# Even mixer: sixteen attention heads as one stream, with the query and key products of each pair of heads woven in

## The chip, the core and the metric

The kernel runs on one core of one Trainium2 chip. The metric is the device time of one execution in microseconds (us). Engines are named as in the profile: PE is TensorE's matmul part and PEld its weight loads, DVE is VectorE, ACT is ScalarE, POOL is GpSimd, SP is SyncE, which here issues nearly all DMAs. Each engine works off its own instructions in the order of the program.

## The reference, cut to what matters

The reference runs a differential attention block with mixture of experts, then two layers with a mixer and a feed-forward each. The change lies in the mixer of the first of these layers (the even mixer), for 512 tokens of width 1024. It projects the normed input once (`even_w_in`) and attends with two sets of eight heads of width 64:

```
q_a, k_a, v_a, q_idx, k_idx, w_idx, q_b, k_b, v_b = split(x @ w_in)
# A: sparse attention. An index score picks 128 keys for each query, softmax over those alone
score = sum_h relu(q_idx[h] . k_idx) * w_idx[h]            # 4 index heads
keep  = top_k(score, 128), within the allowed chunks
o_a   = softmax(where(keep, q_a . k_a / 8, -1e30)) @ v_a    # 8 heads, rotary q and k
# B: chunked attention with a relative position bias
o_b   = softmax(q_b . k_b / 8 + rel_bias) @ v_b             # 8 heads
h     = h + concat(o_a, o_b) @ w_out
```

All arithmetic is in float32 precision. Products are made in three passes of halves (high by high, low by high, high by low).

## The kernel before

Eight stages follow each other; `stage_c` is the even mixer, from about 620 to 941 us of the profiled execution. The stage `stage_e` (the odd mixer, later) uses the same helper for its softmax heads.

**Products.** `fm` makes tiles of 128 outputs x 512 tokens; a tile of the input projection is 8 k-chunks x 3 passes = 24 matmuls of 512 columns into one `mm` buffer of PSUM, one of `w_out` 4 x 3 = 12. The weights are loaded (`wr`), cast to a high half on ACT (`wh`, L110) and the low half is subtracted on DVE (`wl`, L111). `tm` makes the value tiles with the tokens as rows. All these come as lists of units, each with a cost; `weave` merges two lists by cost, `emit` runs a list. What is emitted is then ordered by a list scheduler, which can move an instruction ahead on its engine where it takes it to be ready sooner.

**Query and key stacks.** `qk_tile` takes a tile of two heads out of PSUM (L773) and, with rotary position, `rot` swaps halves by four DMAs into `rsw` (L391), multiplies twice on POOL (L392, L393) and adds on DVE (L394). `q_stack` and `k_stack` split a tile into halves `nh` and `nl` (L654, L655) and lay them by DMA into stacks of 128 rows, so that two matmuls give a full precision score. `rsw`, `nh` and `nl` have one buffer each, and `rsw` shares that of `nh`. `prep` makes the stacks of a pair of heads at once: 12 DMAs.

**Index.** `index_score` makes the index scores; `pick` takes 16 rounds for a block of queries, each round MAX8 (L889) and MATCH_REPLACE8 (L890) on DVE over the 256, 384 or 512 allowed keys; two rounds stand in one unit. Query block 0 needs no rounds, so there are 48 rounds.

**Softmax heads.** `soft_heads` cuts a head into four query blocks i of 128, with n = 128(i+1) keys. A unit t holds `score` of block t, `turn` of block t-2 and `value` of block t-4 (the pair `SOFT`). `score`: two matmuls per block (`s`, L700, two PSUM buffers), bias and row minimum on DVE (L703), exponential with its sum on ACT (L704), reciprocal (L705) and division (L706) on DVE. `turn`: i+1 transposes into the one PSUM buffer `t` (L715) and a copy to `ptall` on ACT (L717). `value`: four matmuls for the whole head (`pv`, L727).

**The order of the stage.** Value and index columns first, the two tiles of index queries, then all tiles of q_b and k_b and v_b, with index scores and the rounds of blocks 1 and 2 woven in; then the eight b heads, with the rounds of block 3, all tiles of q_a and k_a and the rest of v_a; then the eight a heads, with the products of `w_out` for the b half (8 tiles of 12 matmuls); at the end the 8 tiles of `w_out` for the a half.

Of the kernel before, what the change touches and what calls it, by code (L numbers as in the profile page):

```python
# [16 lines left out]
BIG = 1e36  # L17
# [6 lines left out]
SOFT, ATT, WIN = (2, 4), (1, 4), (2, 4)  # L24
# [57 lines left out]
class K:  # L82
# [303 lines left out]
    def rot(self, pool, dst, src, c, s):  # L386

        nc = self.nc
        sw = pool.tile([P, T], F32, name="rsw", tag="nh", bufs=1)
        for b in range(4):  # L390
            nc.sync.dma_start(sw[32 * b:32 * b + 32], src[32 * (b ^ 1):32 * (b ^ 1) + 32])  # L391
        nc.gpsimd.tensor_tensor(sw, sw, s, op=OP.mult)  # L392
        nc.gpsimd.tensor_tensor(src, src, c, op=OP.mult)  # L393
        self.after(4, lambda: nc.vector.tensor_tensor(dst, src, sw, op=OP.add))  # L394
# [292 lines left out]
    def soft_heads(self, pool, heads, begin):  # L687
# [3 lines left out]
        sbs, pts, pvs = {}, {}, {}  # L691

        def score(u, i):
            hd = heads[u]
            if i == 0:
                hd["begin"]()
            n = P * (i + 1)
            s = self.pst()
            for m, (q, k) in enumerate(hd["qk"](i, n)):
                nc.tensor.matmul(s[:, :n], lhsT=q, rhs=k, start=m == 0, stop=m == 1)  # L700
            sb = sbs[u, i] = pool.tile([P, T], F32, name="sb", tag="sb", bufs=self.nsb)
            st = pool.tile([P, 3], F32, name="st", tag="st", bufs=6)
            nc.vector.tensor_tensor_reduce(sb[:, :n], s[:, :n], hd["bias"](i, n), 1.0, 3e38, OP.add, OP.min, st[:, 0:1])  # L703
            nc.scalar.activation(sb[:, :n], sb[:, :n], AF.Exp, bias=st[:, 0:1], scale=-1.0, accum_out=st[:, 1:2])  # L704
            nc.vector.reciprocal(st[:, 2:3], st[:, 1:2])  # L705
            nc.vector.tensor_scalar(sb[:, :n], sb[:, :n], st[:, 2:3], None, op0=OP.mult)  # L706

        def turn(u, i):
            n = P * (i + 1)
            if i == 0:  # L710
                pts[u] = pool.tile([P, 13, P], F32, name="ptall", tag="ptall", bufs=2)
            sb = sbs.pop((u, i))
            tp = self.ptt()
            for j in range(i + 1):
                nc.tensor.transpose(tp[:, j * P:(j + 1) * P], sb[:, j * P:(j + 1) * P], self.ident)  # L715

            nc.scalar.copy(pts[u][:, i:4 * i + 1:3], tp[:, :n].rearrange("p (a b) -> p a b", b=P))  # L717

        def value(u, i):
            if i != NT - 1:  # L720
                return
            e = u % 2
            if e == 0:
                pvs[u // 2] = self.pvt()
            pv, pt = pvs[u // 2], pts.pop(u)
            for j in range(NT):
                nc.tensor.matmul(pv[64 * e:64 * e + 64, j * P:], lhsT=heads[u]["v"](j), rhs=pt[:, 4 * j:3 * j + 4],  # L727
                                 start=j == 0, stop=j == NT - 1, skip_group_check=True)
            if e == 1:
                heads[u]["done"](u // 2, pvs.pop(u // 2))  # L730
# [3 lines left out]
        for t in range(len(us) + SOFT[1]):  # L734
            parts = [(f, us[t - d], c) for f, d, c in ((score, 0, 0.11), (turn, SOFT[0], 0.11), (value, SOFT[1], 0.3))
                     if 0 <= t - d < len(us)]

            def fn(parts=parts, t=t):
                if t == 0:
                    begin()  # L740
# [13 lines left out]
    def stage_c(self):  # L754
# [3 lines left out]
        self.nsb, self.nst, self.nsl = 4, 3, 3  # L758
        with tc.tile_pool(name="pc", bufs=1) as pc:
# [4 lines left out]
            wv = w.rearrange("(k p) n -> p k n", p=P)  # L764
            va = pc.tile([P, NT, 512], F32, name="va", tag="v", bufs=2)
# [4 lines left out]
            def qk_tile(name, c0, n, scale, rope):  # L770
                def done(m, ps):
                    t = pc.tile([P, T], F32, name=name, tag="qk", bufs=8)
# [4 lines left out]
                    if (name, m) == ("kb", 0):  # L777
                        self.after(2, lambda: prep("b", 0))
                return self.fm(w[:, c0:c0 + n], x, done)
# [3 lines left out]
            def prep(kind, c):  # L783

                q, _ = self.q_stack(pc, QK.pop(("q" + kind, c)))
                k = self.k_stack(pc, QK.pop(("k" + kind, c)))
                for e in range(2):
                    stacks[kind, 2 * c + e] = q[e], *k[e]
# [30 lines left out]
            def index_keys():  # L819
# [4 lines left out]
                kq = pc.tile([P, NT, 64], F32, name="kq")  # L824
# [24 lines left out]
            self.emit(qk_tile("qi", 1536, 256, 1.0, True))  # L849
            self.flush()  # L850
# [11 lines left out]
            def index_score(i, hh):  # L862
                def fn():
                    n = P * (i + 1)
                    if hh == 0:
                        scs[i] = pc.tile([P, T], F32, name="sc", tag="sc", bufs=2)
# [16 lines left out]
            def pick(i, rounds):  # L883
                def fn():
                    n = P * (i + 1)
                    sc = scs[i]
                    for r in rounds:
                        m8 = pc.tile([P, 8], F32, name="m8", tag="m8", bufs=2)
                        nc.vector.max(m8, sc[:, :n])  # L889
                        nc.vector.match_replace(sc[:, :n], m8, sc[:, :n], MARK)  # L890
                        if r == 15:
                            nc.vector.tensor_scalar(keep[:, ko[i]:ko[i] + n], sc[:, :n], MARK, BIG, op0=OP.not_equal,
                                                    op1=OP.mult)
                return (0.3 * (i + 1), fn)

            vb = pc.tile([P, NT, 512], F32, name="vb", tag="v", bufs=2)
# [4 lines left out]
            index, late = [], []  # L901
            for i in range(1, NT):
                index += [index_score(i, hh) for hh in range(4)]
                (index if i < NT - 1 else late).extend(pick(i, range(r, r + 2)) for r in range(0, 16, 2))
            proj = (qk_tile("qb", 1860, 512, -0.125, False) + qk_tile("kb", 2372, 512, 1.0, False)
                    + self.tm_cols(w, 2884, 512, x, dvb))
            self.emit(proj[:2])
            self.emit(self.weave(index, proj[2:]))
            yb, ya, mbs = [], [], {}

            def rel_bias(hh):
                def fn():
                    for q in range(hh + (hh > 0), min(8, hh + 2)):
                        make_bias(q)
                    if hh % 2:
                        prep(*(("b", hh // 2 + 1) if hh < 7 else ("a", 0)))
# [10 lines left out]
            def head(kind, hh, v, begin, bias, y):  # L927
                def qk(i, n):
                    q, *k = stacks[kind, hh]
                    return [(q[:, i * P:(i + 1) * P], t[:, :n]) for t in k]  # L930
                return {"qk": qk, "bias": bias, "v": lambda j: v[:, j, hh * 64:hh * 64 + 64], "begin": begin, "done": self.y_out(y)}

            rel = self.soft_heads(pc, [head("b", hh, vb, rel_bias(hh), lambda i, n, hh=hh: mbs[hh][:, T - n:T], yb)
                                       for hh in range(8)], lambda: yb.extend([self.x8("ybh"), self.x8("ybl")]))
            self.emit(self.weave(rel, self.weave(late, qk_tile("qa", 0, 512, -0.125, True)
                                                 + qk_tile("ka", 512, 512, 1.0, True)) + va_units(0, d0)))
            more = lambda hh: lambda: prep("a", hh // 2 + 1) if hh % 2 and hh < 7 else None
            dsa = self.soft_heads(pc, [head("a", hh, va, more(hh), lambda i, n: keep[:, ko[i]:ko[i] + n], ya)
                                       for hh in range(8)], lambda: ya.extend([self.x8("yah"), self.x8("yal")]))
            self.emit(self.weave(dsa, self.fm(w_out[512:1024], lambda k: (yb[0][:, k], yb[1][:, k]), self.add_h), tail=1))  # L940
            self.emit(self.fm(w_out[0:512], lambda k: (ya[0][:, k], ya[1][:, k]), self.last_add))


    def stage_e(self):
# [3 lines left out]
        self.nsb, self.nst, self.nsl = 4, 4, 2  # L948
        with tc.tile_pool(name="pe", bufs=1) as pe:
# [167 lines left out]
            self.emit(self.weave(window, proj[2:]))  # L1117
            heads = [{"qk": lambda i, n, hh=hh: [(q[:, i * P:(i + 1) * P], k[:, :n]) for q, k in stacks[hh]],
                      "bias": lambda i, n: cm[:, T - n:T], "v": lambda j, hh=hh: vc[:, j, hh * 64:hh * 64 + 64],
                      "begin": lambda hh=hh: prep(hh // 2 + 1) if hh % 2 == 0 and hh < 6 else None,  # L1120
                      "done": self.y_out(yc)} for hh in range(8)]
            forg = self.soft_heads(pe, heads, lambda: yc.extend([self.x8("ych"), self.x8("ycl")]))
# [607 lines left out]
```

## Time and profile before

| | us |
|---|---|
| three runs of the kernel | 1907.06, 1909.3, 1910.37 (median 1909.3) |
| profiled execution, its own time | 1910.65 |
| its span, first to last instruction | 1908.9 |
| mean granted clock of TensorE | 0.988 |
| PE busy | 1835.4 (96%) |
| DVE busy | 1318.4 (69%) |
| ACT busy | 978.0 (51%) |
| POOL busy | 226.3 (12%) |

The profiled execution is 1.35 us over the median. A busy PE here is not a full PE: a matmul of 512 columns is booked with about 0.39 us while the next one starts 0.23 us after it, so a short wait between two matmuls hides under the booked time. How much work a stretch holds is therefore counted in matmuls and the distance of their starts, not read from the busy share alone.

### The profile page before, as it was taken

The numbers are of one execution on the slowest core, as the hardware profiler recorded it, in microseconds if no ns is written. First come the engines' busy times: TensorE is split into PE (matmuls) and PEld (weight loads), VectorE is DVE, ScalarE is ACT, GpSimd is POOL, SyncE is SP. The second block draws the span as 40 slices with busy tenths as digits, with TensorE's granted clock in tenths as the row PEclk, the third lists the DMA queues.
The fourth block names the chain that finished last, engine by engine and source line by source line (L and its number), as shares of the span: only waits on it lengthen the run. The fifth ranks groups of instructions, "written<-read, shape, count | busy, mean of one in ns | idle before, by whom it ended". The sixth has DMA issues, their size and how long they took to land.

```text
span 1908.9 us, 24634 instructions
## 1 busy us (share of the span) xinstructions
PE 1835.4 (96%) x8604; PEld 1448.6 (76%) x8605; DVE 1318.4 (69%) x2815; ACT 978.0 (51%) x1663; POOL 226.3 (12%) x277
## 2 busy tenths in 40 slices
PE   8999997999998999998999999999999999999997
PEld 6767685778887876675688888888777788888885
DVE  6586848999998689756677447744576667537753
ACT  5565656888885325346454224433376544324442
POOL 2000012222322302310200000012200100000001
PEclk9999998999999999999999999999999999999998
DMA  5511157999994454454232343234545233243331
GB/s 190 181 45 67 67 172 268 355 369 370 368 366 147 135 148 115 111 147 106 83 96 75 91 114 107 68 95 141 137 112 133 67 90 103 77 119 89 88 85 60
DMA packets 260098, 274.74 MB, mean 144 GB/s; under 512 B 14438, under 2 KB 175622, under 8 KB 259968
## 3 DMA queue, kind: packets, MB, share of 16 engines
q1 hardware_dynamic: 250688, 257.56, 44.1%
q0 software_dynamic: 5072, 10.00, 1.5%
q10 hardware_dynamic: 4208, 5.56, 0.8%
q8 instruction: 69, 1.13, 0.2%
q14 instruction: 61, 0.50, 0.1%
HBM read 238.19 MB, written 15.73 MB: 133 GB/s over the span
## 4 chain that ended last, share of the span: by engine, by line
PE 51%; DVE 2%; ACT 2%; DMA 1%; POOL 1%; SPq 1%; issue 1%; DVEq 0%; POOLq 0%; ACTq 0%
PE mm L137 14%; PE mm L135 14%; PE mm L136 14%; PE pv L727 2%; PE t L715 1%; PE s L700 1%; PE pv L1101 1%; PE mm L140 1%; PE mm L139 1%; PE mm L141 1%; DMA rsw<-qd 0%; SPq L391 0%; POOL rsw L392 0%; PE s L1067 0%; PE t L1086 0%
## 5 line engine op out<-in xcount | busy, mean ns | idle before, releaser
L110 ACT CAST wh<-wr 128x1024 fp32r<-128x1024 f32 (+5 forms) x335 | 306.6, 916 | 442.6 <-PE mm L136 318.8
L111 DVE TENSOR_TENSOR wl<-wr,wh 128x1024 fp32r<-128x1024 f32 (+4 forms) x332 | 356.8, 1078 | 196.4 <-ACT wh L110 193.7
L135 PE MATMUL mm<-xh,wh 128*128 128x512 f32 x952 | 372.9, 392 | 2.1 <-DVE h L384 1.8
L137 PE MATMUL mm<-xh,wl 128*128 128x512 f32 x952 | 372.9, 392 | 0.2 <-DVE wl L111 0.2
L136 PE MATMUL mm<-xl,wh 128*128 128x512 f32 x952 | 371.8, 391 | 0.0
L135 PEld LDWEIGHTS mm<-xh,wh 128*128 128x128 f32 x952 | 179.2, 188 | 40.0 <-issue 3.5
L137 PEld LDWEIGHTS mm<-xh,wl 128*128 128x128 f32 x952 | 179.1, 188 | 38.1 <-issue 1.1
L136 PEld LDWEIGHTS mm<-xl,wh 128*128 128x128 f32 x952 | 179.1, 188 | 36.1 <-issue 0.2
L111 DVE TENSOR_TENSOR wl<-wx,wh 128x1024 fp32r<-128x1024 f32 x123 | 151.3, 1247 | 11.7 <-ACT wh L110 5.6
L110 ACT CAST wh<-wx 128x1024 fp32r<-128x1024 f32 x134 | 139.5, 1050 | 27.6 <-PE mm L141 23.4
L139 PE MATMUL mm<-wh,xh 128*128 128x512 f32 (+2 forms) x352 | 132.0, 380 | 9.7 <-ACT wh L110 5.6
L135 PE MATMUL mm<-hh,wh 128*128 128x512 f32 x352 | 139.0, 395 | 0.0
L136 PE MATMUL mm<-hl,wh 128*128 128x512 f32 x352 | 138.9, 395 | 0.0
L137 PE MATMUL mm<-hh,wl 128*128 128x512 f32 x352 | 138.9, 395 | 0.0
L140 PE MATMUL mm<-wl,xh 128*128 128x512 f32 (+2 forms) x352 | 131.1, 373 | 4.3 <-DVE wl L111 4.2
L141 PE MATMUL mm<-wh,xl 128*128 128x512 f32 (+2 forms) x352 | 129.7, 369 | 0.0
L624 DVE TENSOR_TENSOR z<-mm,rb 128x512 f32<-128x512 f32 x88 | 60.4, 688 | 81.3 <-PE mm L137 81.3
L139 PE MATMUL mm<-wh,xeh 128*128 128x512 f32 x256 | 103.9, 406 | 0.8 <-ACT xeh L1361 0.8
L277 POOL TENSOR_TENSOR acc<-acc,sq 128x512 f32<-128x512 f32 x42 | 58.3, 1388 | 377.2 <-ACT sq L273 376.8
L141 PE MATMUL mm<-wh,xel 128*128 128x512 f32 x256 | 101.8, 398 | 0.0
L140 PE MATMUL mm<-wl,xeh 128*128 128x512 f32 x256 | 101.1, 395 | 0.0
L384 DVE TENSOR_TENSOR h<-mm,h 128x512 f32<-128x512 f32 x88 | 60.5, 690 | 50.4 <-PE mm L137 49.3
(406 smaller groups left out, 3352.3 us busy)
## 6 DMA issues: line engine op xcount, KB each, us to landing
wr<-in_ffn_w_up SPq DMA_DIRECT2D x88, 512.0 KB, 4.9
wx<-in_moe_w_gate SPq DMA_DIRECT2D x23, 1024.0 KB, 8.9
wx<-in_moe_w_up SPq DMA_DIRECT2D x22, 1024.0 KB, 9.7
wx<-in_moe_w_down SPq DMA_DIRECT2D x22, 1024.0 KB, 11.0
wr<-in_ffn_w_down SPq DMA_DIRECT2D x32, 704.0 KB, 4.6
wr<-in_da_w_in SPq DMA_DIRECT2D x11, 1024.0 KB, 5.1
wr<-in_even_w_in SPq DMA_DIRECT2D x11, 1024.0 KB, 5.5
wr<-in_moe_w_up SPq DMA_DIRECT2D x10, 1024.0 KB, 8.0
```

What stands on the lines that cost most here:

```text
L110: nc.scalar.copy(h, raw)
L111: (nc.gpsimd if eng else nc.vector).tensor_tensor(l, raw, h.bitcast(F32), op=OP.subtract)
L135: mm(out, lhsT=wh, rhs=xh, start=first, stop=False, skip_group_check=True)
L136: mm(out, lhsT=wh, rhs=xl, start=False, stop=False, skip_group_check=True)
L137: mm(out, lhsT=wl, rhs=xh, start=False, stop=last, skip_group_check=True)
L139: mm(out, lhsT=xh, rhs=wh, start=first, stop=False, skip_group_check=True)
L140: mm(out, lhsT=xh, rhs=wl, start=False, stop=False, skip_group_check=True)
L141: mm(out, lhsT=xl, rhs=wh, start=False, stop=last, skip_group_check=True)
L277: nc.gpsimd.tensor_tensor(self.acc, self.acc, sq, op=OP.add)
L384: self.nc.vector.tensor_tensor(self.h[:, m], ps, self.h[:, m], op=OP.add)
L624: nc.vector.tensor_tensor(z[:, 2:], ps, self.rb, op=OP.mult)
L727: nc.tensor.matmul(pv[64 * e:64 * e + 64, j * P:], lhsT=heads[u]["v"](j), rhs=pt[:, 4 * j:3 * j + 4], start=j == 0, stop=j == NT - 1, skip ...
```

## The change

All of it lies in `stage_c`, `soft_heads`, `halves` and `rot`; `stage_e` is only adapted to the new arguments, and the order of its instructions is the same on every engine as before.

- The sixteen heads are one list of units, b heads first. Beside each two heads stands the pair of query and key tiles that is wanted two heads later (for heads 0 to 7 the rest of the rounds, one per unit, and the rest of v_a too); beside heads 12 to 15 stands `w_out` of the b half.
- Input tiles are made 128 columns at a time, in units of 2 k-chunks, so that a quarter of a tile is woven in and not a whole one. Each load brings one tile.
- Before the first head now come only the first two pairs of q_b and k_b, v_b, the index scores and 18 rounds.
- Division moves from DVE (L706) to ACT (`norm`, an activation Copy with the reciprocal as its scale), one unit after the score. `turn` comes three and `value` five units after it.
- In a heads, blocks 1 and 3 are transposed into one of the four `mm` buffers, so that two buffers take turns.
- Stacks of a pair are made in two steps, the query's at block 0 and the key's at block 2 of the odd head; `nh` and `nl` have two buffers, and `rsw` one of its own. There are five `sb` buffers and not four.
- The delay before the rotary addition is emitted is 6 and not 4; `kq` shares the buffer of `hk`; the first tile of a outputs uses a value buffer.

```diff
+        one, two, three = lags
...
             nc.vector.reciprocal(st[:, 2:3], st[:, 1:2])
-            nc.vector.tensor_scalar(sb[:, :n], sb[:, :n], st[:, 2:3], None, op0=OP.mult)
+            if one is None:
+                nc.vector.tensor_scalar(sb[:, :n], sb[:, :n], st[:, 2:3], None, op0=OP.mult)
+            sts[u, i] = st
+
+        def norm(u, i):
+            sb, st = sbs[u, i][:, :P * (i + 1)], sts.pop((u, i))
+            nc.scalar.activation(sb, sb, AF.Copy, scale=st[:, 2:3])
...
-            tp = self.ptt()
+            tp = self.mmt() if i % 2 and heads[u].get("spare") else self.ptt()
...
-        sw = pool.tile([P, T], F32, name="rsw", tag="nh", bufs=1)
+        sw = pool.tile([P, T], F32, name="rsw", tag="rsw" if self.nhl > 1 else "nh", bufs=1)
...
-        h = pool.tile([P, T], F32R, name="nh", tag="nh", bufs=1)
-        l = pool.tile([P, T], F32R, name="nl", tag="nl", bufs=1)
+        h = pool.tile([P, T], F32R, name="nh", tag="nh", bufs=self.nhl)
+        l = pool.tile([P, T], F32R, name="nl", tag="nl", bufs=self.nhl)
...
-        self.nsb, self.nst, self.nsl = 4, 3, 3
+        self.nsb, self.nst, self.nsl, self.nhl = 5, 3, 3, 2
...
-                return self.fm(w[:, c0:c0 + n], x, done)
+                return self.fm(w[:, c0 + m * P:c0 + m * P + P], x, done, sub=2)
...
-            self.emit(self.weave(index, proj[2:]))
+            self.emit(first[4:])
+            self.emit(self.weave(index + picks[:18], self.tm_cols(w, 2884, 512, x, dvb) + pair["b"](1)))
+            picks = picks[18:]
...
+                nxt = (kind, hh // 2 + 1) if hh < 7 else ("a", 0) if kind == "b" else None
+                return {} if hh % 2 == 0 or nxt is None else {0: lambda: prep(*nxt, 0), 2: lambda: prep(*nxt, 1)}
...
-            self.emit(self.weave(rel, self.weave(late, qk_tile("qa", 0, 512, -0.125, True)
-                                                 + qk_tile("ka", 512, 512, 1.0, True)) + va_units(0, d0)))
...
-            self.emit(self.weave(dsa, self.fm(w_out[512:1024], lambda k: (yb[0][:, k], yb[1][:, k]), self.add_h), tail=1))
...
+            beside(8, pair["b"](2), 6)
+            beside(8, pair["b"](3), 6)
+            beside(8, pair["a"](0), 6)
+            beside(8, pair["a"](1) + va_units(0, d0), len(picks))
+            beside(8, pair["a"](2))
+            beside(8, pair["a"](3))
+            out = self.fm(w_out[512:1024], lambda k: (yb[0][:, k], yb[1][:, k]), self.add_h, sub=2)
+            beside(8, out[:6])
+            beside(8, out[6:12])
+            beside(len(att), out[12:])
```

What this makes of the order, at three places. On PE, among the a heads, before (`s` scores, `t` transposes, `pv` values, `mm<-y...` products of `w_out`):

```order
L700 MATMUL s<-kh,qs 128x128
L715 MATMUL t<-ident,sb 128x128
L137 MATMUL mm<-yah,wl 128x512
L700 MATMUL s<-kl,qs 128x128
L715 MATMUL t<-ident,sb 128x128 x2
L700 MATMUL s<-kh,qs 128x256
L700 MATMUL s<-kl,qs 128x256
L715 MATMUL t<-ident,sb 128x128 x3
L700 MATMUL s<-kh,qs 128x384
L700 MATMUL s<-kl,qs 128x384
L700 MATMUL s<-kh,qs 128x512
L715 MATMUL t<-ident,sb 128x128 x4
```

And PE among the a heads now (`mm<-xh,wh` and its two fellows are the woven query and key products, `mm<-ident` the transposes in the second buffer):

```order
L703 MATMUL s<-kh,qs 128x256
L703 MATMUL s<-kl,qs 128x256
L724 MATMUL t<-ident,sb 128x128 x3
L703 MATMUL s<-kh,qs 128x384
L703 MATMUL s<-kl,qs 128x384
L724 MATMUL mm<-ident,sb 128x128 x4
L135 MATMUL mm<-xh_7149,wh 128x512
L136 MATMUL mm<-xl_7151,wh 128x512
L137 MATMUL mm<-xh_7149,wl 128x512
L135 MATMUL mm<-xh_7149,wh 128x512
L136 MATMUL mm<-xl_7151,wh 128x512
L137 MATMUL mm<-xh_7149,wl 128x512
```

Before, scores and transposes follow each other with hardly a product between; now six or twelve products stand after every one or two blocks.

On DVE, among the b heads, before (`ISA sb,st<-s,mb` is bias and minimum, `m` and `sc` the rounds):

```order
L705 RECIPROCAL st<-st 128x1
L703 ISA sb,st<-s,mb 128x512
L703 ISA st 128x1
L706 TENSOR_SCALAR sb<-sb,st 128x384
L889 MAX m_8364<-sc 128x8
L705 RECIPROCAL st<-st 128x1
L111 TENSOR_TENSOR wl<-wr,wh 128x1024
L890 MATCH_REPLACE sc<-m_8364,sc 128x512
L706 TENSOR_SCALAR sb<-sb,st 128x512
L703 ISA sb,st<-s,mb 128x128
```

And DVE among the b heads now:

```order
L708 RECIPROCAL st<-st 128x1
L706 ISA sb,st<-s,mb 128x256
L706 ISA st 128x1
L902 MATCH_REPLACE sc<-m_8595,sc 128x512
L655 TENSOR_TENSOR nl<-qb,nh 128x512
L708 RECIPROCAL st<-st 128x1
L706 ISA sb,st<-s,mb 128x384
L706 ISA st 128x1
```

The division is gone from DVE, and the rounds still stand between the steps of the softmax.

On ACT, among the b heads, before (`sb,st<-sb,st` is the exponential, `ptall` the copy of the transposes):

```order
L704 ACTIVATE sb,st<-sb,st 128x256
L110 CAST wh<-wr 128x1024
L717 COPY ptall<-t 128x4x128
L717 COPY ptall<-t 128x128
L749 CAST ybh<-pv 128x512
```

And ACT among the b heads now (`sb<-sb,st` is the division):

```order
L707 ACTIVATE sb,st<-sb,st 128x256
L715 ACTIVATE sb<-sb,st 128x256
L726 COPY ptall<-t 128x4x128
L707 ACTIVATE sb,st<-sb,st 128x384
L715 ACTIVATE sb<-sb,st 128x384
L110 CAST wh<-wr 128x1024
L726 COPY ptall<-t 128x128
```

ACT has one instruction more for each block, and in some places the division stands right behind the exponential of the same block.

## Rows read from the trace of the kernel before

**Rows 1.** Busy time of each engine in stretches (start:end, length), count in brackets, clock
```profile
727.00:800.00 73.00, 65.46 (x297) 45.50 (x297) 66.74 (x177) 33.42 (x83) 24.06 (x21) 1.00 0.42 107
800.00:856.00 56.00, 55.27 (x290) 44.19 (x289) 30.81 (x69) 22.10 (x50) 10.59 (x8) 1.00 0.53 146
856.00:916.00 60.00, 50.99 (x229) 29.22 (x228) 33.90 (x138) 36.69 (x107) 0.34 (x1) 1.00 0.40 97
1441.00:1501.00 60.00, 60.00 (x292) 40.33 (x291) 42.49 (x151) 40.68 (x113) 0.00 (x0) 1.00 0.39 95
```

**Rows 2.** The same for instructions on the tile mm alone: PE, PEld, DVE, ACT
```profile
727.00:856.00 129.00, 85.28 (x376) 64.18 (x375) 10.28 (x15) 1.80 (x4) 1.00 0.47 124
856.00:916.00 60.00, 7.95 (x25) 4.35 (x25) 0.67 (x1) 0.00 (x0) 1.00 0.40 97
1441.00:1501.00 60.00, 26.51 (x90) 15.21 (x88) 4.82 (x7) 0.53 (x1) 1.00 0.39 95
```

**Rows 3.** The same for line 715, the transposes: PE, PEld
```profile
856.00:916.00 60.00, 15.53 (x80) 8.77 (x80) 1.00 0.40 97
1441.00:1501.00 60.00, 14.65 (x80) 9.29 (x80) 1.00 0.39 95
```

**Rows 4.** Groups on PE from 1441 to 1501: count, busy, mean ns, idle
```profile
L727 PE MATMUL pv<-ptall,vc 128*64 128x512 f32 (+3 forms) x58 | 18.5, 448 | 0.0
```

**Rows 5.** PE in order of time: start, us, engine, line, shape; two pairs of neighbours
```profile
628.01 0.29 PE L141 MATMUL mm<-wh,xl 128*128 128x290 f32 x1
628.14 0.29 PE L139 MATMUL mm<-wh,xh 128*128 128x290 f32 x1
...
675.27 0.39 PE L135 MATMUL mm<-xh,wh 128*128 128x512 f32 x1
675.50 0.39 PE L136 MATMUL mm<-xl,wh 128*128 128x512 f32 x1
```

**Rows 6.** Start of the index scores: SP and PE in order of time
```profile
657.70 2.41 SPq L391 DMA_DIRECT2D rsw<-qi  x4
668.30 1.10 SPq L668 DMA_DIRECT2D qis<-nl  x2
670.62 0.36 PE L871 MATMUL s<-kih,qis 128*128 128x256 f32 x1 [1.82 <-DMA qis<-nl]
```

**Rows 7.** Engines in the stretch after that start; clock is the seventh number
```profile
671.20:674.60 3.40, 3.40 (x11) 2.72 (x10) 2.49 (x4) 0.70 (x2) 0.00 (x0) 0.50 0.96 327
```

**Rows 8.** PE's waits from 640 to 950: us, times, longest
```profile
PE t L715 <- ACT ptall L717: 5.1, 10, 0.7
PE s L700 <- DVE st L703: 2.7, 2, 2.3
PE t L715 <- DVE sb L706: 2.3, 3, 1.1
PE s L700 <- DMA kl<-nl: 1.0, 1, 1.0
```

**Rows 9.** Groups of instructions from 640 to 950: count, busy, mean ns, idle before
```profile
L704 ACT ACTIVATE sb<-sb,st 128x128 f32<-128x128 f32 (+1 forms) x64 | 35.8, 561 | 12.5 <-DVE st L703 9.6 <-DVE st L705 2.7
L706 DVE TENSOR_SCALAR sb<-sb,st 128x128 f32<-128x128 f32 (+1 forms) x64 | 29.8, 472 | 0.6
L889 DVE MAX8 m<-sc 128x8 f32<-128x384 f32 x16 | 8.9, 558 | 0.3
L890 DVE MATCH_REPLACE8 sc<-m,sc 128x384 f32<-128x384 f32 x16 | 8.7, 542 | 0.0
L110 ACT CAST wh<-wr 128x1024 fp32r<-128x1024 f32 x24 | 25.3, 1053 | 64.3 <-PE mm L136 44.6 <-PE mm L141 9.8 <-DVE m L889 4.4
L111 DVE TENSOR_TENSOR wl<-wr,wh 128x512 fp32r<-128x512 f32 x16 | 11.4, 714 | 4.7 <-ACT wh L110 4.5
L384 DVE TENSOR_TENSOR h<-mm,h 128x512 f32<-128x512 f32 x16 | 11.0, 690 | 9.7 <-PE mm L137 9.7
```

**Rows 10.** DMA issues on the profile's page: count, KB each, median us to landing
```profile
wr<-in_ffn_w_up SPq DMA_DIRECT2D x88, 512.0 KB, 4.9
```

More of the change, by code (lines that the diff above doesn't have):

```diff
@@ L393, in rot @@
         nc.gpsimd.tensor_tensor(src, src, c, op=OP.mult)
-        self.after(4, lambda: nc.vector.tensor_tensor(dst, src, sw, op=OP.add))
+        self.after(6, lambda: nc.vector.tensor_tensor(dst, src, sw, op=OP.add))
     def stage_a(self):
@@ L729, in value, with fn @@
             if e == 1:
-                heads[u]["done"](u // 2, pvs.pop(u // 2))
+                heads[u]["done"](u // 2 % 4, pvs.pop(u // 2))
         us = [(u, i) for u in range(len(heads)) for i in range(NT)]
         units = []
[L734 to L740, printed above, removed]
+        for t in range(len(us) + three):
+            parts = [(f, us[t - d], c) for f, d, c in ((score, 0, 0.11), (norm, one, 0.0), (turn, two, 0.11), (value, three, 0.3))
+                     if d is not None and 0 <= t - d < len(us)]
+            def fn(parts=parts):
                 for f, u, _ in parts:
@@ L886, in fn @@
                     sc = scs[i]
[L887 to L893, printed above, removed]
@@ L911, in rel_bias, with dsa_done @@
+            def dsa_done(c, pv):
+                if c % 2 == 0:
+                    ya.append(self.x8("ya") if c else pc.tile([P, 4, T], F32R, name="ya", tag="v", bufs=2))
+                t = ya[-1][:, 2 * (c % 2):2 * (c % 2) + 2]
+                nc.scalar.copy(t[:, 0], pv)
+                nc.vector.tensor_tensor(t[:, 1], pv, t[:, 0].bitcast(F32), op=OP.subtract)
             def rel_bias(hh):
@@ L925, in rel_bias, with ahead, head @@
                 return fn
-            def head(kind, hh, v, begin, bias, y):
+            def ahead(kind, hh):
+                nxt = (kind, hh // 2 + 1) if hh < 7 else ("a", 0) if kind == "b" else None
+                return {} if hh % 2 == 0 or nxt is None else {0: lambda: prep(*nxt, 0), 2: lambda: prep(*nxt, 1)}
+            def head(kind, hh, v, begin, bias, done):
                 def qk(i, n):
-                    q, *k = stacks[kind, hh]
+                    q, *k = stacks[kind + str(hh)]
@@ L937, in stage_c @@
-            more = lambda hh: lambda: prep("a", hh // 2 + 1) if hh % 2 and hh < 7 else None
-            dsa = self.soft_heads(pc, [head("a", hh, va, more(hh), lambda i, n: keep[:, ko[i]:ko[i] + n], ya)
-                                       for hh in range(8)], lambda: ya.extend([self.x8("yah"), self.x8("yal")]))
-            self.emit(self.weave(dsa, self.fm(w_out[512:1024], lambda k: (yb[0][:, k], yb[1][:, k]), self.add_h), tail=1))
-            self.emit(self.fm(w_out[0:512], lambda k: (ya[0][:, k], ya[1][:, k]), self.last_add))
+                return {"qk": qk, "bias": bias, "v": lambda j: v[:, j, hh * 64:hh * 64 + 64], "begin": begin, "done": done,
+                        "spare": kind == "a", "at": ahead(kind, hh)}
@@ new lines, in stage_c, with beside @@
+            att = self.soft_heads(pc, [head("b", hh, vb, rel_bias(hh), lambda i, n, hh=hh: mbs[hh][:, T - n:T], rel_done)
+                                       for hh in range(8)]
+                                  + [head("a", hh, va, lambda: None, lambda i, n: keep[:, ko[i]:ko[i] + n], dsa_done)
+                                     for hh in range(8)], (1, 3, 5))
+            def beside(n, units, picked=0):
+                nonlocal att, picks
+                a, att, b, picks = att[:n], att[n:], picks[:picked], picks[picked:]
+                self.emit(self.weave(self.weave(a, b) if b else a, units))
```

78 lines of the change are left out of this document (44 added, 34 removed).

## The prediction

> **What bounds the kernel now.** I first read the engines' busy time by stretches of the stage, because the share over the whole span says little. In [rows 1] the reader sees four stretches. From 727 to 800 (b heads with the rounds) DVE is 66.74 of 73 us busy and PE waits; from 800 to 856 (b heads without rounds) PE is nearly full; from 856 to 916 (the a heads) PE has 50.99 of 60, and neither DVE (33.90) nor ACT (36.69) is near full: there the heads wait on their own chain of score, softmax, transpose. The last stretch lies in the odd mixer, which uses the same helper with products beside every head, and PE is full, 60.00 of 60. It is my measure of what a head costs PE if it never has to wait.
>
> Busy PE time hides waits, so I count. A product of 512 columns takes 0.227 us from start to start and one of 290 takes 0.135, by two pairs of neighbours (0.23 and 0.13) and their runs [rows 5]. In the odd stretch stand 90 products [rows 2], 90 x 0.227 = 20.4 us, so 39.6 us are heads. It has 80 transposes [rows 3], ten per head: 8 heads. Their 64 value matmuls would be complete but for six [rows 4]; at 18.5/58 = 0.319 each these add 1.9. (39.6 + 1.9)/8 = 5.2 us per head.
>
> With this price, what PE loses before:
> - a heads: 80 transposes [rows 3] are 8 heads, 41.6 us, and 25 products [rows 2] 5.7 us: 47.3 of 60, so 12.7 lost.
> - b heads: 376 products [rows 2], of which 96 (the values' columns) have 290 columns: 280 x 0.227 = 63.6, 96 x 0.135 = 12.9, 8 heads 41.6: 118.1 of 129, so 10.9 lost. The waits there are PE's on a score buffer that DVE empties late (2.7 us in two), on the division (2.3) and on stack DMAs (1.0) [rows 8].
> - start of the index scores: PE waits 1.82 us for the stack `qis` [rows 6], and then runs 3.40 us at a granted clock of 0.50 [rows 7], the lower level of 1.2 GHz where 2.4 is full: half of 3.4 is lost, 1.7. Together 3.5.
>
> The pot is 12.7 + 10.9 + 3.5 = 27.1 us. The matmuls are the same in number before and after, so the change can win this, or lose what new waits take.
>
> **The change, part by part.** *Where the products stand.* By the order, 192 + 96 products now stand beside heads 0 to 7 (192 of 512 columns, 96 of 290) and 192 beside heads 8 to 15. PE's work is then 41.6 + 43.6 + 12.9 = 98.1 us in the first half and 41.6 + 43.6 = 85.2 in the second. The a heads, whose chain left PE idle, get 167 products more, some 38 us of cover, in pieces of six to twelve between blocks. If no other engine is late, the 12.7 and 10.9 go to nothing. The question is how much DVE, ACT and the DMAs give back.
>
> *DVE, heads 0 to 7.* Before it worked 66.74 + 30.81 = 97.55 us in the b heads [rows 1]. It loses 32 divisions of 0.472 [rows 9] = 15.1, and 7.3 fewer weight and output tiles pass through it, at 0.714 (`wl`) and 0.690 (the addition to h) [rows 9] = 10.3. It gains 14 rounds of blocks 1 and 2 that were woven in earlier, at 0.558 + 0.542 [rows 9] = 15.4. 97.55 - 15.1 - 10.3 + 15.4 = 87.6 of 98.1, 89%. At 91% in the stretch to 800 PE lost most of its time on DVE, but there two rounds stood in one unit and products came by whole tiles; now one round stands per unit and the scores of a unit come five units ahead of its values. I take 4 us given back, between 0 and 10 (what was lost before in all of the b heads).
>
> *ACT.* It gets 64 divisions. The trace has none on ACT; the nearest row is the exponential of the same tile, 0.561, then DVE's division, 0.472, and as the far end the cast of a full 1024 columns, 1.053 [rows 9]. At 0.561 they are 18.0 per half. Heads 0 to 7: 33.42 + 22.10 [rows 1] + 18.0 = 73.5 of 98.1 (75%). Heads 8 to 15: 36.69 [rows 1] + 18.0 + 12 more weight casts at up to 1.053 [rows 9] (12.6) = 67.3 of 85.2 (79%). Even at 1.053 the divisions add 15.7 more per half, 89.2 and 83.0, still under PE. What is added is also a wait: the division stands on ACT until the reciprocal is done, and behind it are queued the next exponential and the copies to `ptall`, for which PE's transposes wait. The division comes one unit later, so mostly the reciprocal is done. I take 2 us, between 0 and 6, in the second half, where the copies already cost PE the most: 5.1 us in ten waits [rows 8].
>
> The Trainium skill speaks against this move: "ScalarE: Activation LUTs", section "Rules for kernel authors", says that an elementwise multiplication belongs on VectorE and not on ScalarE, and section "What ACT_TABLE_LOAD costs" gives an activation with one [128,1] operand about 280 ns and 0.833 ns per column. That would be an estimate of 547 ns on the mean of 128 to 512 columns, and the trace agrees in direction, 561 against 472 [rows 9]; by its price the sum would be the same.
>
> *Stacks and their DMAs.* Two `nh`, two `nl` and an own `rsw` mean that the six DMAs of a step need not wait for those of the step before, and by the order the casts stand six and more blocks ahead of the first score that wants them. The stack wait of the b heads (1.0 for `kl` [rows 8]) goes; it is in the 10.9.
>
> *Start of the index scores.* Only 96 products stand ahead of the first index score, and 120 did before: PE arrives 24 x 0.227 = 5.4 us sooner. Against that, the swap of the first tile was issued at 657.70, but its stack only at 668.30 [rows 6], because `nh` waited for the second tile's `rsw` in the same buffer. With buffers of their own, the stack can be laid soon after the rotation, and POOL no longer has the bias tiles ahead of it. I expect the first stack in time and the stack of the third index head about 1 us late. Of the 3.5 us I count 2.0 won (1.0 wait, some half clock left); the bounds are all 3.5 won, or 5.4 - 1.8 = 3.6 more lost, if the stack comes no sooner than before.
>
> *Costed at nothing.* Single tile loads are 512 KB, which land in 4.9 us [rows 10], with 24 x 0.227 = 5.4 us of PE per tile and three buffers; without that cover the first tile of a pair would cost up to 4.9. The fifth `sb`, the delay of 6, `kq` in the buffer of `hk` and the output tile in a value buffer only shift work on engines with slack. A quarter tile holds its `mm` buffer longer; one is filled, one emptied, so two are left for the transposes.
>
> **Sum.** 27.1 - 1.5 (index) - 4 (DVE) - 2 (ACT) = 19.6 us less. The span goes from 1908.9 to 1889.3, the profiled execution from 1910.65 to 1891.0; the median of the runs lay 1.35 under that, so 1889.7, rounded to 1890.
>
> **Rivals.**
> - *DVE becomes the bound of heads 0 to 7* (faster, less). Each reciprocal follows the exponential of its own block, and if DVE stands for it about 0.7 us (the exponential's 0.561 and some handover) 32 times, that is 22.4 on 87.6 = 110.0, 11.9 over PE's 98.1. Then 27.1 - 1.5 - 11.9 - 2 = 11.7 are won: 1898. For it: the rounds now lie beside the heads where DVE was already full. Against: the order still puts rounds or tiles between exponential and reciprocal, and DVE's idle before the division was 0.6 in all [rows 9]. Chance 0.15.
> - *ACT becomes the bound, slower than before.* Where the division stands right behind its own exponential (14 of 64 places by the order), or where DVE is late with the reciprocal, ACT stands still, and the copies behind it hold PE. With a wait of w per division ACT reaches PE's time at w = (85.2 - 67.3)/32 = 0.56 in the a heads and at (98.1 - 73.5)/32 = 0.77 in the b heads. Past both the loss is 64 w - 42.5, and the gain (27.1 - 1.5 = 25.6) is gone at w = 1.06. A reciprocal behind one subtraction and one round (0.714 + 0.542 [rows 9]) waits about 1.2: 34.3 lost, 8.7 slower in sum, 1918. For it: ACT already idled 9.6 us for the minimum from DVE [rows 9], and now depends on DVE twice per block. Against: 50 of 64 divisions have a unit between. Chance 0.08.
> - *The products do not fill the gaps.* The wait for the one `t` buffer stays in all b heads and in the even blocks of the a heads: 48 turns. At 5.1/10 = 0.51 us [rows 8] each, 24.5 us: a gain of 1.1, 1908, no change. For it: the copy to `ptall` is on ACT, which gets fuller. Against: in the odd mixer PE is full with the same one buffer [rows 1]. Chance 0.07.
>
> **How the numbers follow.** My forecast has 0.70. Its bounds: all 27.1 won and 2 us for the roundness of the 5.2 us price, 1880; both give-backs (10 and 6) and the late stack (7.1) leave 4 of the 27.1, 1905. The range 1880 to 1904 takes in the first rival and leaves out the other two, 0.15, and little of my own case. A measurement of this kernel tells 0.2%, 3.8 us, from no change: the forecast and the first rival are faster (0.85), the last rival is the same (0.07), the second slower (0.08).
>
> **What would show it.** Right: in the a heads PE's idle time is gone and the stretch holds some 190 products, and their eight heads take about 87 us; the stage's last heads end some 20 us sooner; DVE about 88 us in the eight b heads and ACT about 67 in the a heads, its division at 0.55. PE's waits on the score buffer and the division fall under 2 us. The first index score waits less than 1.8 us. Wrong: waits of ACT on the reciprocal that PE shares through the copies, DVE above 95% in the b heads, a longer wait at `qis`, or a clock at 0.50 in a place that was full before. A gain outside this stage would be against all that I say, since the other stages' order is unchanged.

## The result, and the profile after

The changed kernel takes 1882.3 us (median of 4 runs, 1879.27 to 1882.52), the kernel before 1909.61 beside it. The ratio is 0.9856, 95% interval 0.9839 to 0.9873: 27.3 us faster, where 19.6 were forecast. The profiled execution took 1882.52 us, its span is 1880.8, 28.1 under that of before.

First the engines' busy time from the first score of head 0 to the first of head 8, and from there to the last value matmul (columns as in [rows 1]):

```profile
702.40:796.40 94.00, 92.23 (x478) 72.48 (x477) 80.08 (x220) 64.37 (x153) 22.26 (x20) 1.00 0.62 153
796.40:883.60 87.20, 87.20 (x420) 63.32 (x418) 44.57 (x133) 60.16 (x154) 10.17 (x8) 1.00 0.48 129
```

PE, which had 50.99 of 60 us in the a heads [rows 1], is full there: 87.20 of 87.20. DVE has 80.1 of 94.0 in the b heads, ACT 60.2 of 87.2 in the a heads. The tile `mm` alone in the same stretches (PE, PEld, DVE, ACT):

```profile
702.40:796.40 94.00, 65.98 (x295) 48.48 (x294) 6.10 (x9) 1.65 (x4) 1.00 0.62 153
796.40:883.60 87.20, 55.68 (x235) 38.29 (x234) 8.28 (x12) 7.66 (x17) 1.00 0.48 129
```

These 530 instructions hold the 48 transposes of the second buffer. By the starts in the trace 480 products lie between the first score (702.4) and the last value matmul (883.6), 96 of them with 290 columns: 12.96 + 87.17 = 100.1 us, which leaves 81.1 for sixteen heads, 5.07 each. Counted so, before (725.7 to 914.7, 402 products) a head took 6.66. That is 25.5 us of the gain.

Now PE's waits from 690 to 890, all of them, against [rows 8] (us, times, longest):

```profile
PE s L703 <- DVE st L706: 1.1, 1, 1.1
PE t L724 <- ACT sb L715: 0.4, 1, 0.4
PE mm L140 <- DVE wl L111: 0.2, 1, 0.2
```

Of the waits on the transposes' copy, the score buffer, the division and the stack DMAs, 11.1 us in [rows 8], 1.5 are left. Third, the index scores, which stood 1.82 us for `qis` and then ran at a granted clock of 0.50 [rows 6, 7]. PE in order of time, and the stretch behind:

```profile
654.31 0.33 PE L852 MATMUL t<-ident,k 128*128 128x128 f32 x1 [2.14 <-DVE k L847]
...
665.26 0.28 PE L884 MATMUL s<-kih,qis 128*128 128x256 f32 x1
```

```profile
665.20:668.60 3.40, 3.40 (x18) 2.84 (x18) 3.05 (x5) 2.64 (x5) 1.08 (x1) 1.00 0.45 108
```

The first score waits for nothing and the clock stays at 1.00, so all 3.5 us are won; but PE comes sooner to the turn of the index keys too and waits 2.14 us there for DVE (0.4 before). Net of that, the time from the stage's start to head 0, less the products that moved out of it, fell by 2.0 us. The tail behind the heads, taken in the same way, fell by 1.5. Together 25.5 + 2.0 + 1.5 = 29.0; the spans differ by 0.9 less. That 0.9 lies outside the stage and says nothing: in the traces of this document the stage begins anywhere from 619.6 to 623.6 us.

What ACT got, in groups from 620 to 930 (count, busy, mean ns, idle before):

```profile
L707 ACT ACTIVATE sb<-sb,st 128x128 f32<-128x128 f32 (+1 forms) x64 | 36.0, 563 | 9.6 <-DVE st L706 9.1
L715 ACT ACTIVATE sb<-sb,st 128x128 f32<-128x128 f32 (+1 forms) x64 | 35.1, 559 | 7.7 <-DVE st L708 7.5
```

A division costs on ACT what an exponential does, 559 ns, as it was priced [rows 9], and ACT stands 7.5 us for reciprocals, while PE's waits on the division are 0.4 us.

### The profile page after: what moved, and what is told of

It is laid out like the page before. It is cut to its first block, busy times and chain, and to the rows that moved or that the text cites. A ratio compares the mean times of both kernels' runs of the same rounds, so it can differ in the third digit from the quotient of the medians.

```text
span 1880.8 us, 24577 instructions
## 1 busy us (share of the span) xinstructions
PE 1822.3 (97%) x8604; PEld 1448.9 (77%) x8605; DVE 1295.7 (69%) x2751; ACT 1006.8 (54%) x1727; POOL 222.2 (12%) x277
## 4 chain that ended last, share of the span: by engine, by line
PE 59%; DVE 4%; DMA 1%; ACT 1%; issue 1%; POOL 1%; SPq 1%; DVEq 0%; POOLq 0%; ACTq 0%
PE mm L135 16%; PE mm L137 16%; PE mm L136 16%; PE pv L736 3%; PE s L703 2%; PE t L724 1%; PE mm L140 1%; DVE wl L111 1%; PE mm L139 1%; PE mm L141 1%; PE pv L1138 1%; DVE sc L902 1%; SPq L391 0%; DVE m L901 0%; DMA rsw<-qd 0%
## 5 line engine op out<-in xcount | busy, mean ns | idle before, releaser
L110 ACT CAST wh<-wx 128x1024 fp32r<-128x1024 f32 x134 | 139.6, 1050 | 28.1 <-PE mm L141 24.1
```

The costliest lines, as they stand in the source:

```text
L110: nc.scalar.copy(h, raw)
```

## The experiments

All but one start from the changed kernel. Where times lie close, I compare a stretch of the profile that can't be touched by the rest of the program: from the first score of head 0 to the row sums (L349) behind the stage's last product, 702.4 to 913.95 = 211.6 us in the changed kernel. The theory at the outset: PE had no products to lie between the blocks of the a heads; the change puts them there, and the other parts are worth little.

### Where the products stand

**No products beside heads 12 to 15.**

```diff
-            beside(8, out[:6])
-            beside(8, out[6:12])
-            beside(len(att), out[12:])
+            self.emit(att)
+            self.emit(out)
```

> The changed kernel, but the 96 products of w_out of the b half are not woven beside heads 12 to 15; they come all together behind the last head. Theory (PE's idle time in the a heads goes because products lie between the blocks): these four heads, bare, lose what a bare head lost before, about 1.7 us each (13.8 us lost in eight a heads by a price of 5.06 us per head, which is what sixteen heads take in the trace of the changed kernel): 5 to 8 us over the changed kernel's 1882.3, so 1887 to 1890, with PE's waits on the transposes' copy or the division back in these heads alone. Rival (the longer distance from score to value and the second buffer for transposes have shortened the chain, the products are not needed): under 2 us, 1884 at most.

Measured 1890.27 us, 8.0 over the changed kernel, the upper edge of the theory; the stretch is 222.3 us, 10.7 longer. The four bare heads and what they wait for (columns as in [rows 1] and [rows 8]):

```profile
834.20:871.60 37.40, 31.61 (x133) 17.22 (x132) 13.77 (x56) 26.22 (x75) 2.50 (x2) 0.91 0.21 50
```

```profile
PE mm L724 <- ACT sb L715: 2.9, 4, 1.2
PE t L724 <- ACT ptall L726: 2.0, 2, 1.2
```

With longer distances and a second buffer a bare head still waits, for the division and the copy, and the mean clock of the stretch falls to 0.91, which the expectation had not counted: 9% of 37.4 us, 3.4 of the 10.7. The rival (under 2 us) is out.

**All parts, but the products where they stood before.** The pairs of a heads go beside the b heads, those of b heads ahead of head 0, nothing beside the a heads:

```diff
-            self.emit(self.weave(index + picks[:18], self.tm_cols(w, 2884, 512, x, dvb) + pair["b"](1)))
+            self.emit(self.weave(index, pair["b"](1) + pair["b"](2) + pair["b"](3) + self.tm_cols(w, 2884, 512, x, dvb)))
...
+            beside(32, va_units(0, d0) + pair["a"](0) + pair["a"](1) + pair["a"](2) + pair["a"](3), len(picks))
...
+            self.emit(att)
+            self.emit(out)
```

> The reverse: division on ACT one unit later, distances of three and five, the second buffer for transposes, two nh, five sb, stacks in two steps, quarter tiles, but the products where the kernel before had them: all query and key tiles of the b heads before the first head, all those of the a heads beside the b heads, and no product at all beside the a heads (w_out of the b half behind them; in the kernel before 33 products lay there). To fit, nl has one buffer, sc two and qk seven. Theory: a bare head loses 1.7 us (the kernel before) to 2.7 (the four bare heads tried), 14 to 21 us over the changed kernel's 1882, so 1896 to 1905. Rival (the parts shorten the chain of a head by themselves): under 1890.

Measured 1901.51 us (ratio to before 0.9958, 0.9943 to 0.9973): inside the theory's range. Without the place of the products the parts win 8 us of 27. The run is not quite the change less the place: `nl` has one buffer in it and not two, and the 33 products that the kernel before had among its a heads are gone too.

### The buffers of the stacks

**One buffer for `nh` and `rsw` together, and one for `nl`.**

```diff
-        self.nsb, self.nst, self.nsl, self.nhl = 5, 3, 3, 2
+        self.nsb, self.nst, self.nsl, self.nhl = 5, 3, 3, 1
```

> The changed kernel with one buffer each for nh and nl, and rsw in that of nh, as before. Theory (the stack of the first index tile comes late again): the wait at the first index score is back, 1.8 us or more, with a stretch at half clock behind it, 3 to 5 us in the stage, 1885 to 1887. Rival (the order of the stage has moved enough that the buffers don't matter): within 1 us.

Measured 1909.49 us, the time of the kernel before (ratio 1.0, 0.999 to 1.0009). Both theory and rival are far off: this one number takes back all of the gain. The theory's place is not where it is lost. The stack of the first index tile is late again (its `nh` is cast at 664.34 us, in the changed kernel at 657.60), but PE does not wait there: its first index score now stands at 669.86 (665.26), behind other products. The trace shows one place where the time goes. In order of time, SP, DVE, ACT and PE around the stacks for heads 12 and 13:

```profile
845.70 2.41 SPq L391 DMA_DIRECT2D rsw<-qa  x4
...
852.27 0.69 DVE L394 TENSOR_TENSOR qa<-qa,rsw 128x512 f32<-128x512 f32 x1 [4.49 <-POOL qa L393]
...
853.48 0.62 ACT L654 CAST nh<-qa 128x512 fp32r<-128x512 f32 x1
...
858.55 0.61 ACT L654 CAST nh<-ka 128x512 fp32r<-128x512 f32 x1
...
860.04 1.10 SPq L682 DMA_DIRECT2D kh<-nh  x2
...
866.75 0.77 PE L703 MATMUL s<-kh,qs 128*128 128x128 f32 x2 [8.53 <-DMA kh<-nh]
```

The swap of the next pair's query tile holds the buffer from 845.7 until its addition ends at 852.96; only then `nh` for this pair can be cast (853.48), and for its key again only when the query's DMAs have left (858.55). PE stands 8.53 us; the clock falls to its lower level while it stands, at 861.5, and stays there until 875.2:

```profile
861.50:875.20 13.70, 7.42 (x23) 5.87 (x24) 3.28 (x17) 5.99 (x19) 1.32 (x2) 0.50 0.60 170
```

In the changed kernel the same steps overlap: the swap of the key tile is issued while the query's `nh` is cast, both at 837.5.

```profile
837.47 0.62 ACT L654 CAST nh<-qa 128x512 fp32r<-128x512 f32 x1
...
837.49 2.44 SPq L391 DMA_DIRECT2D rsw<-ka  x4
...
845.31 0.62 ACT L654 CAST nh<-ka 128x512 fp32r<-128x512 f32 x1 [0.42 <-DVE ka L394]
```

This place costs 8.5 us of standing and, of the 8.4 us from 866.75 to 875.2 in which PE works at half clock, about half: some 12.7 of the 27 together. The rest I read from the order, not from a run of its own: the list scheduler puts products ahead, and both heads of a pair behind them. Products on PE between the first scores of heads 7 to 15, counted in the program's order (first score of head 7 to that of 8, and so on):

| | 7 to 8 | 8 to 9 | 9 to 10 | 10 to 11 | 11 to 12 | 12 to 13 | 13 to 14 | 14 to 15 |
|---|---|---|---|---|---|---|---|---|
| changed | 84 | 24 | 24 | 24 | 18 | 18 | 18 | 18 |
| one buffer | 118 | 8 | 43 | 5 | 24 | 0 | 33 | 3 |
| nothing but the place (below) | 128 | 12 | 49 | 13 | 66 | 14 | 14 | 0 |

The even heads of the a set are bare again, though the program asks for products beside them.

**Nothing but the place of the products.** All other parts undone:

```diff
-                return {} if hh % 2 == 0 or nxt is None else {0: lambda: prep(*nxt, 0), 2: lambda: prep(*nxt, 1)}
+                return {} if hh % 2 == 0 or nxt is None else {0: lambda: (prep(*nxt, 0), prep(*nxt, 1))}
...
-                        "spare": kind == "a", "at": ahead(kind, hh)}
+                        "spare": False, "at": ahead(kind, hh)}
...
-                                     for hh in range(8)], (1, 3, 5))
+                                     for hh in range(8)], (None, 2, 4))
```
and one `nh` with four `sb` buffers as above, and whole tiles (no `sub=2`).

> The changed kernel with nothing left of the change but where the products stand: division on DVE in the score's unit, transposes two and values four units later, all transposes in the buffer t, one buffer each for nh and nl with rsw in that of nh, four sb buffers, both stacks of a pair made at once, whole tiles. Each of these alone has cost 0 to 2.4 us. Theory (the place of the products is the change; the rest are conveniences): 1882 to 1888. Rival (each part covers for the others, all gone together the waits come back): 1892 or more.

Measured 1906.51 us (ratio 0.999, 0.998 to 1.0). The theory is wrong, the rival right in its time, though "each part covers" is not what happens, since one part, the buffers, takes back the whole gain by itself. That each part alone costs 0 to 2.4 us was not known of the buffers, and the run above shows it to be wrong. What the place alone would be worth this run can't say: here too the products do not stand where the program asks for them (last row of the table). PE's waits from 800 to 915:

```profile
PE t L724 <- ACT ptall L726: 4.3, 5, 1.5
PE s L703 <- DMA kh<-nh: 1.5, 1, 1.5
PE mm L135 <- ACT ya L928: 1.4, 2, 0.7
```

So my theory had to be mended: products in the gaps win the time, and in both runs with shared buffers they did not stay beside every head. That they leave because the stacks of the next pair are late is read from the place above and from the order; no run separates it. Not tried: `rsw` by itself and the second `nh` by itself.

### The division on ACT

**The kernel before with this edit alone**, directly behind the exponential, in the even mixer (`nst` is 3 there and 4 in the odd one):

```diff
-            nc.vector.tensor_scalar(sb[:, :n], sb[:, :n], st[:, 2:3], None, op0=OP.mult)
+            if self.nst == 3:
+                nc.scalar.activation(sb[:, :n], sb[:, :n], AF.Copy, scale=st[:, 2:3])
+            else:
+                nc.vector.tensor_scalar(sb[:, :n], sb[:, :n], st[:, 2:3], None, op0=OP.mult)
```

> The kernel before with one edit: in the even mixer the division is on ACT, directly behind the exponential as it stood on DVE. Theory (the move alone is worth little, the weaving is what wins): the b heads win up to 4 us on DVE, the a heads lose 2 to 6 because ACT stands for each reciprocal and the copies behind it are late: 1906 to 1913. Rival 1 (DVE's relief is the gain): 1900 or less. Rival 2 (ACT becomes the bound): over 1914.

Measured 1921.11 us (ratio 1.0068, 1.0047 to 1.0088): slower than the theory's range, and in that of rival 2. The eight a heads take 72.3 us against 61.6 (853.1 to 914.7) before; the b heads 127.8 against 127.4. The stretch of the a heads, and the longest of PE's waits in it:

```profile
849.80:922.10 72.30, 58.77 (x242) 32.27 (x240) 27.14 (x109) 49.95 (x139) 0.00 (x0) 0.93 0.37 88
```

```profile
PE t L718 <- ACT ptall L720: 8.2, 12, 1.3
PE s L700 <- DVE st L703: 2.2, 5, 0.6
```

```profile
L707 ACT ACTIVATE sb<-sb,st 128x128 f32<-128x128 f32 (+3 forms) x32 | 17.3, 558 | 0.9 <-DVE st L705 0.9
```

ACT is busy 49.95 of 72.3, so it is no bound by its sum, and it stands only 0.9 us for reciprocals. But the divisions, 17.3 us, stand in its queue ahead of the copies for which PE waits (8.2 us, and 4.3 in these heads before), and the clock falls to a mean of 0.93: 7% of 72.3 us, 5.1, about half of the 10.7 lost. In bare heads the move is a loss.

That the b heads take as long as before does not show that DVE's relief is worth nothing there. They hold one stand that the kernel before does not have, at a stack in the one buffer `nh`; the clock is at 0.50 from about 807 to 814:

```profile
808.90 0.62 ACT L654 CAST nh<-kb 128x512 fp32r<-128x512 f32 x1 [7.54 <-DMA qs<-nh]
...
811.02 0.61 PE L139 MATMUL mm<-wh,xh 128*128 128x290 f32 x1 [5.60 <-DVE ka L776]
```

An estimate of what this costs is 5.60 us and half of the 3.4 that PE works at the lower clock, some 7. So much shorter than before the b heads would be without it; 2.0 of it are the two stack waits of the kernel before, which are gone here. What DVE's relief is worth in the old order stays open.

**The division directly behind the exponential, in the changed kernel:** the distances `(1, 3, 5)` become `(0, 3, 5)`.

> The changed kernel with the division, still on ACT, directly behind the exponential in the same unit (0 units after the score, not 1). In the kernel before, the same place of the division cost 9.8 us in the stage. Theory (the distance of one unit is what keeps ACT from standing for the reciprocal; with products woven in PE has some cover for it, not for all): 2 to 6 us more from the first score to the stage's end, 1884 to 1888. Rival 1 (products cover it wholly): within 1 us. Rival 2 (the wait is the same as in the kernel before): 9 us or more.

Measured 1883.25 us; the stretch is 211.5 us, as before the edit. ACT's waits for the reciprocal, 7.5 us in sixteen in the changed kernel, grow, and PE's waits are the same 1.1 and 0.4 us:

```profile
ACT sb L715 <- DVE st L708: 10.0, 20, 1.5
```

Rival 1 is right: in the changed kernel the division directly behind the exponential costs nothing that these runs can tell. (Its transposes also come a unit later than in the kernel before; with two units and the division one unit later, below, nothing was lost either.)

**The division back on DVE,** one unit after the score:

```diff
-            nc.scalar.activation(sb, sb, AF.Copy, scale=st[:, 2:3])
+            nc.vector.tensor_scalar(sb, sb, st[:, 2:3], None, op0=OP.mult)
```

> The changed kernel with the division back on DVE, at the same place in the program (one unit after the score). Theory (DVE's relief matters only in the b heads, where it is fullest): DVE's 80.1 us there grow by 32 x 0.472 = 15.1 to 95.2, over the 94.0 us that PE takes, so 1 to 6 us lost there and nothing in the a heads: 1883 to 1888. Rival (PE waited little on DVE, so ACT's relief counts as much): no change or faster, 1880 to 1883.

Measured 1880.13 us (1878.64 to 1883.41), which can't be told from the changed kernel; the stretch is 212.5 us, 0.9 longer. The b heads:

```profile
699.30:794.30 95.00, 92.64 (x479) 72.41 (x478) 90.96 (x252) 50.70 (x123) 21.09 (x20) 1.00 0.61 151
```

DVE is 91.0 of 95.0 us busy, 96%, and PE waits 2.3 us in all of the heads (1.7 in the changed kernel), 1.2 of it in one place where the changed kernel waits 0.2:

```profile
PE mm L140 <- DVE wl L111: 1.2, 1, 1.2
```

So the move to ACT is not where the gain is; nor does it cost. The Trainium skill, in "ScalarE: Activation LUTs", section "Rules for kernel authors", would leave this multiplication on VectorE. In the order of the kernel before the run agrees, by 12 us, though by the queue and the clock as told above; between products the runs can't tell the two apart.

### Parts that can be undone

**Distances two and four** (`(1, 2, 4)` for `(1, 3, 5)`).

> The changed kernel with transposes two and values four units after the score, where it has three and five. From the first score of head 0 to the end of the last product of the stage the changed kernel's trace takes 211.6 us. Theory (the one unit more is what covers the division's way over DVE and ACT): PE waits on the division before its transposes, 2 to 6 us in that stretch, 1884 to 1888. Rival (products between the blocks cover it anyway): within 1 us, 1882 to 1883.

Measured 1882.85 us, the stretch 211.9: nothing is lost, as the rival said.

**One buffer for transposes** (`"spare": False`).

> The changed kernel with all transposes in the one buffer t, also those of blocks 1 and 3 of the a heads. Theory (with products between the blocks the copy is done before the next transposes come): 0 to 2 us more, 1882 to 1884, PE's waits on the copy under 1 us. Rival (the second buffer is what removed the 5.1 us of waits on the copy): 4 to 5 us more, 1886 to 1887.

Measured 1883.56 us, the stretch 212.1, PE's waits on the copy 0.2 us: 0.5 is lost, as the theory said.

**Whole tiles** (no `sub=2`, and `out[:3]`, `out[3:6]`, `out[6:]`).

> The changed kernel with whole tiles woven in (24 products, or 12 of w_out, in one piece) where it has quarters of 6. Theory (what counts is that products stand after every block or two; with whole tiles about half of the blocks stand bare): 2 to 7 us more from the first score to the stage's end, 1884 to 1889, with waits on the copy and the division. Rival (one large piece per four blocks is cover enough): within 1 us.

Measured 1884.32 us, the stretch 214.0: 2.4 us are lost, in the theory's range. Its waits are not there: PE waits 0.2 us on the copy and once 1.9 on the score buffer, where the changed kernel waits 1.1. Where the other 1.4 us go, the list of waits does not show.

**All rounds beside the heads** (`index` for `index + picks[:18]`, then 12 rounds per pair).

> The changed kernel with all 48 rounds beside the b heads; it has 18 of them beside the index scores before. DVE is 80.1 of 94.0 us busy in the b heads of the changed kernel; with the division on DVE it was 91.0 of 95.0 and PE lost only about 1 us. 16 rounds over 256 keys and 2 over 384 add some 18 us: 98 of 94. Theory (DVE bounds from 100% on): 3 to 8 us more, 1885 to 1890, PE's waits on the score buffer. Rival (the rounds only move, the stretch before the heads gets shorter by as much): within 1 us.

Measured 1882.4 us, but this tested nothing: the scheduler moved the rounds back. From 703.3 to 797.7 the trace has 29 of them, and 28 in the changed kernel:

```profile
L901 DVE MAX8 m<-sc 128x8 f32<-128x512 f32 (+1 forms) x29 | 18.2, 630 | 0.4
```

**Keys turned later** (`self.after(13, turn_keys)` for 10).

> The changed kernel with the transposes of the index keys emitted three cost units later (13 for 10), so that some 14 products more stand ahead of them. In the changed kernel PE waits 2.1 us there for DVE's last step on the keys. Theory: this wait goes and nothing takes its place, as the first index score comes 10 us later: 2 us less, 1880. Rival (the keys' halves are late for the first index score): the wait moves there, 1882.

Measured 1881.37 us, the whole stage unchanged within 0.2 us. The 2.1 us at the keys are gone, and PE waits 1.35 us elsewhere: at the third index score, for the cast of the second tile of index queries, and not, as the rival had it, at the first one for the keys. Either way the gain goes to the next wait:

```profile
663.92 0.28 PE L884 MATMUL s<-kih,qis 128*128 128x256 f32 x1
...
670.04 0.36 PE L884 MATMUL s<-kih,qis 128*128 128x256 f32 x1 [1.35 <-ACT nh L654]
```

## Why the prediction was right, and where its sizes were off

*The bound and the pot.* PE's lost time in the heads was the right thing to count, and by that price nearly all of it was won: a head came out at 5.07 and not 5.2 us, which makes the heads' pot 25.5 us instead of 23.6. (The 5.07 is read from the changed kernel, so waits left in its heads are inside it.) The measured 1882.3 lies near the fast end of the range, 1880, because the 6 us set aside for DVE and ACT were not needed.

*DVE's give-back, 4 us forecast, none seen.* The term rested on DVE's 91% in the stretch to 800 [rows 1]. DVE came to 80.1 of 94.0, and even at 91.0 of 95.0 (division back on DVE) the stretch lost 0.9 us. So in the new order a DVE as full as that does not hold PE, and the first rival falls with it. What held PE in the b heads before stays open: in the run that relieved DVE in the old order the stand of 5.60 us hides it.

*ACT's give-back, 2 us forecast, 0.4 seen.* ACT worked 60.2 us and not 67.3, and its waits for reciprocals hardly reach PE.

*The rival on the slower side* came close to something real, in another kernel and for another reason: in the kernel before, the division on ACT makes 1921 us, where the rival had 1918 for the changed one. But the rival had ACT stand 1.2 us for each reciprocal, and there it stood 0.9 us for 32; the divisions themselves and the clock made the loss. That the two times are close is luck. With products beside the heads even the same place of the division costs nothing, so it is not the unit between, on which I had argued, that takes this rival away. In bare heads ACT's queue is on the chain; between products it has room.

*Stacks.* That the stack wait of the b heads goes was right (there were two of 1.0, one for `kh` beside that for `kl`) and missed the point. I asked what the second buffers remove from the old order, and not what the new order would be without them: 27 us. The mechanism that I forecast, products in the gaps, is therefore only half of what the runs show.

*Index.* 2.0 us forecast and 2.0 won, but not as worked out, so the agreement is luck: the expected wait of 1 us for the third index head did not come, all 3.5 were won, and 2.1 went to a wait on the keys that the sum did not have. The expected wait stands behind this one: in the last experiment it comes, with 1.35 us.

*The sum.* 1.9 (price of a head) + 4 + 2 (give-backs) + 1.5 (tail) = 9.4 us over the forecast 19.6, and 29.0 is what the stage lost by the two profiled executions; their spans show 28.1 and the medians 27.3, a difference within the scatter of what lies outside the stage.

## What to carry to other kernels

Count what a stretch of the bottleneck holds before asking which engine is full: waiting heads beside a stock of independent products are worth their whole loss. When work is moved beside other work, ask first which buffers both now use at the same time; going back to shared buffers for the stacks took back everything here. And judge an engine's move in its new surroundings: the same division was 12 us of loss in the old order and nothing between products.

## What the runs showed of the hardware

In bare heads the clock also fell after short waits, and not in every kernel. In the kernel before, the a heads lost 12.7 us at a clock of 1.00 [rows 1]. With the division on ACT, where PE's longest wait in them was 1.3 us, the mean was 0.93. In the kernel with nothing but the place of the products a piece of the a heads ran at 0.50, the lower level:

```profile
894.20:901.00 6.80, 6.29 (x22) 4.30 (x20) 4.85 (x22) 5.06 (x17) 0.00 (x0) 0.50 0.12 29
```

Ahead of it lay waits of 1.54 and 0.80 us for stack DMAs, and before these several of 0.6 to 0.7 us for ACT. PE works 6.29 of the 6.80 us; half of that, about 3.1, is lost, more than the two waits for DMAs took.
